# Gated recurrence block: gate, output and sum stores move from SyncE's queue to those of ScalarE and GpSimd, and a weight moves to another ring

## The chip, the core and the metric

The kernel runs on one core of a Trainium2 chip. Its time is the device time of one execution in microseconds; each kernel is run several times and the median is taken. A profile is one more execution, recorded by the hardware profiler.

The engines are TensorE (PE, with PEld for its weight loads), VectorE (DVE), ScalarE (ACT), GpSimd (POOL) and SyncE (SP). Each works through its own instructions in order and waits at semaphores. A DMA is started by an instruction on the queue of SP, ACT or POOL; if that instruction has to wait, everything behind it on the same queue waits too.

## The reference

One decoder block over 1024 tokens of width 1024, in float32. What matters here is the mixer:

```python
proj = x @ w_in                   # q | f | i | og | pool_v | gate_a | gate_b
f = lb + (1 - lb) * sigmoid(f_pre);  k = 1 - f
o = hgrn2_chunked(q, k, i, log f)              # 8 heads of 128, S_t = diag(f_t) S_(t-1) + k_t v_t^T
o = o * rsqrt(mean(o*o) + eps) * g * sigmoid(og)
a = o @ w_a
pooled = causal_multiscale_pool(pool_v)        # 4 groups, windows 2, 4, 8, 16
b = (pooled @ w_pool per group) * pool_scale
mix = (sigmoid(gate_a) * a + sigmoid(gate_b) * b) @ w_out
x = LN(alpha * x + mix);  x = LN(alpha * x + relu(x @ w_up)**2 @ w_down)
```

## The kernel before

Every float32 operand is split in two parts: ACT casts the high part (L118), DVE subtracts it from the source for the low part (L119), and PE makes three products of the parts (L201, L203, L204; in `mm3` L105, L106, L107). The big products are made in pairs of 128 output columns by a scheme with seven block products instead of eight (`pair`); `run` issues them, `takes` are the functions that receive a finished block: a gate's `put` applies the sigmoid (L696) and stores the tile to DRAM (L699 gates a and b, as `ga` and `gb`; L680 the output gates `og`).

A loop over 8 heads, two halves of 512 tokens each, makes the recurrence `hgrn(h, u)`. It begins with the decay `fd` in the ring `tA` (a scan on DVE, L811; reciprocals L817). GpSimd takes every sixteenth column of it as `T` (L819) and makes a few small tiles of that (to L838). DVE, ACT and PE go on with them: the transposes L870, ACT's copy L872, the state product L875, DVE's state `st` (L880, L883), the scores L887 and L898, their masked copy `att` (L905), the output products L915 and L918. ACT then squares (L923), takes a root (L924) and scales (L928); PE transposes (L931); DVE multiplies by the gate into the gate's own tile `og` (L932), which is stored to DRAM as `o` (L933).

Between the heads stand other pieces, listed in `EXTRAS`: `pooled` makes the window means and stores them as `po` (L754); `gates`; `o_sums` loads four tiles of `o` (L594), makes sums of them on DVE (L608 to L611) and stores them as `s1` to `s4` (L613) for the later product with w_a; `pool_products` loads a group's w_pool (L716) and its pooled tiles (L594), splits both, multiplies them (L105 to L107), scales by the gate on DVE (L729) and stores `pb` (L730). The pooled tiles use the rings `og` and `v`, the split of w_pool `q` and `f`. The rings named here have two buffers each (`tA`, `og`, `v`, `raw`; `q` and `f` have three); a tile that takes a buffer waits until the last use of the tile before it there, a store's landing among them.

A scheduler sets the order on each engine from the dependences, the priorities and its own estimate of when things are ready; after that the order is fixed. The last recurrence, head 7's second half, has a high priority. All stores and loads named here are on SP's queue.

## Time and profile before

| | us |
|---|---|
| three runs | 1462.3, 1462.83, 1464.97 |
| median | 1462.83 |
| profiled execution | 1460.19 |
| its span in the profile | 1458.5 |
| busy: PE, DVE, ACT, POOL | 1436.4, 1141.6, 758.3, 58.6 |

The span is the time from the first to the last instruction that the profiler recorded; the rest of the execution's time lies around it. [...] In the rows of the profile, a line such as L118 is the line of the kernel, `w<-og` is what is written and read, by the names of the tiles without their numbers; the granted clock (PEclk) is 1.00 when TensorE runs at full speed.

### The profile page before, as it was taken

Reading aid. Unit: us, or ns where it says so; the run is one execution under the profiler, and the core shown is the slowest. Engines: PE = TensorE matmul, PEld = TensorE weight load, DVE = VectorE, ACT = ScalarE, POOL = GpSimd, SP = SyncE. Lnnn points to the kernel's source line nnn. Section 1 sums busy time; section 2 is a strip of 40 time slices with the busy share of each in tenths; the row PEclk is TensorE's granted clock in tenths of the full one; section 3 lists DMA queues with packets and bytes.
Section 4 is the critical chain, followed back from the end, with each engine's and each line's share of the span. In section 5 each row is a group of like instructions: output and inputs, shape, how many; then the busy total and the mean of one; then the engine's idle time right before and its main releaser. Section 6 shows DMA issues by size and latency. Waiting matters only on the chain.

```text
span 1458.5 us, 20662 instructions
## 1 busy us (share of the span) xinstructions
PE 1436.4 (98%) x7377; PEld 1187.9 (81%) x7377; DVE 1141.6 (78%) x1838; ACT 758.3 (52%) x1383; POOL 58.6 (4%) x244
## 2 busy tenths in 40 slices
PE   8999999999999998999999999999999999999997
PEld 7888888888888886788888878888888888888886
DVE  5967989899898885768985597666666787777977
ACT  5445565666656655556542376555555443333535
POOL 0001001001000010000002100000000100000000
PEclk9999999999999999999999999999999999999999
DMA  7232233323234447897672225444474874445322
GB/s 253 70 126 87 85 98 101 109 75 114 90 99 138 152 132 249 301 299 241 223 247 99 73 94 195 159 146 144 152 261 149 275 260 150 153 141 163 130 73 116
DMA packets 160615, 226.82 MB, mean 156 GB/s; under 512 B 11232, under 2 KB 84480, under 8 KB 160512
## 3 DMA queue, kind: packets, MB, share of 16 engines
q1 hardware_dynamic: 158576, 218.93, 44.7%
q0 software_dynamic: 1152, 4.19, 0.8%
q10 hardware_dynamic: 784, 2.38, 0.5%
q8 instruction: 58, 0.95, 0.3%
q14 instruction: 45, 0.37, 0.1%
HBM read 154.16 MB, written 71.30 MB: 155 GB/s over the span
## 4 chain that ended last, share of the span: by engine, by line
PE 94%; DVE 3%; DMA 1%; ACT 1%; issue 0%; SPq 0%; DVEq 0%
PE ps_pj L201 16%; PE ps_pj L203 16%; PE ps_pj L204 16%; PE ps_pj L1283 4%; PE ps_pj L1285 4%; PE ps_pj L1284 4%; PE ps_pj L106 3%; PE ps_pj L107 3%; PE ps_pj L105 2%; PE ps_tr L1285 1%; PE ps_tr L1283 1%; PE ps_tr L1284 1%; PE ps_sc L201 1%; PE ps_sc L203 1%; PE ps_sc L204 1%; PE ps_hg L203 1%
## 5 line engine op out<-in xcount | busy, mean ns | idle before, releaser
L201 PE MATMUL ps_pj<-act,w 128*128 128x512 f32 x1068 | 421.6, 395 | 0.4 <-ACT act L123 0.2
L203 PE MATMUL ps_pj<-act,w 128*128 128x512 f32 x1068 | 415.1, 390 | 0.5 <-DVE act L124 0.5
L204 PE MATMUL ps_pj<-act,w 128*128 128x512 f32 x1068 | 414.1, 390 | 0.0
L201 PEld LDWEIGHTS ps_pj<-act,w 128*128 128x128 f32 x1068 | 200.6, 188 | 42.8 <-ACT act L123 0.6
L204 PEld LDWEIGHTS ps_pj<-act,w 128*128 128x128 f32 x1068 | 200.5, 188 | 42.3
L203 PEld LDWEIGHTS ps_pj<-act,w 128*128 128x128 f32 x1068 | 200.6, 188 | 40.6 <-DVE act L124 0.9
L118 ACT CAST w<-t 128x512 fp32r<-128x512 f32 x170 | 104.7, 620 | 105.0 <-PE ps_pj L203 53.8
L118 ACT CAST w<-raw 128x512 fp32r<-128x512 f32 x143 | 88.2, 620 | 117.3 <-PE ps_pj L203 62.5
L119 DVE TENSOR_TENSOR w<-raw,w 128x512 fp32r<-128x512 f32 x143 | 99.8, 702 | 55.2 <-ACT w L118 53.9
L119 DVE TENSOR_TENSOR w<-t,w 128x512 fp32r<-128x512 f32 x170 | 115.9, 685 | 29.6 <-ACT w L118 29.4
L1245 ACT CAST act<-act 128x1024 fp32r<-128x1024 f32 x66 | 66.9, 1050 | 107.9 <-issue 35.0
L1246 DVE TENSOR_TENSOR act<-act,act 128x1024 fp32r<-128x1024 f32 x66 | 79.3, 1220 | 18.5 <-ACT act L1245 15.8
L1285 PE MATMUL ps_pj<-act,act 128*128 128x512 f32 x240 | 92.9, 389 | 0.0
L1284 PE MATMUL ps_pj<-act,act 128*128 128x512 f32 x240 | 92.9, 389 | 0.0
L1283 PE MATMUL ps_pj<-act,act 128*128 128x512 f32 x240 | 92.4, 389 | 0.0
L275 DVE TENSOR_TENSOR c<-c,ps_pj 128x512 f32<-128x512 f32 x95 | 64.5, 681 | 18.0 <-PE ps_pj L204 13.4
L271 ACT COPY c<-ps_pj 128x512 f32<-128x512 f32 x96 | 55.2, 582 | 12.8 <-PE ps_pj L204 12.8
L817 DVE RECIPROCAL tC<-tA 128x128 f32<-128x128 f32 x64 | 54.1, 904 | 0.0
L1284 PEld LDWEIGHTS ps_pj<-act,act 128*128 128x128 f32 x240 | 45.1, 188 | 9.4
L1285 PEld LDWEIGHTS ps_pj<-act,act 128*128 128x128 f32 x240 | 45.1, 188 | 9.4
L1283 PEld LDWEIGHTS ps_pj<-act,act 128*128 128x128 f32 x240 | 45.1, 188 | 9.3
L241 DVE TENSOR_TENSOR t<-raw,raw 128x512 f32<-128x512 f32 x43 | 29.6, 689 | 21.9 <-DMA raw<-in_w_in_dram 19.7
(415 smaller groups left out, 2719.8 us busy)
## 6 DMA issues: line engine op xcount, KB each, us to landing
h<-c SPq DMA_DIRECT2D x106, 256.0 KB, 2.1
act<-h SPq DMA_DIRECT2D x78, 256.0 KB, 2.9
raw<-in_w_in_dram SPq DMA_DIRECT2D x64, 256.0 KB, 3.4
draw<-in_w_down_dram SPq DMA_DIRECT2D x16, 1024.0 KB, 7.8
raw<-in_w_up_dram SPq DMA_DIRECT2D x30, 512.0 KB, 4.2
raw<-in_w_in_dram SPq DMA_DIRECT2D x18, 512.0 KB, 4.0
hf<-h SPq DMA_DIRECT2D x34, 256.0 KB, 2.9
c<-o SPq DMA_DIRECT2D x24, 256.0 KB, 3.4
```

Source lines behind the costliest of these rows:

```text
L118: A.copy(hi, src)
L119: V.tensor_sub(lo, src, f(hi))
L201: PE.matmul(ps, wh[:, k], th, start=first and k == 0, stop=False, skip_group_check=True)
L203: PE.matmul(ps, wh[:, k], tl, start=False, stop=False, skip_group_check=True)
L204: PE.matmul(ps, wl[:, k], th, start=False, stop=k == CH - 1, skip_group_check=True)
L271: A.copy(t, ps)
L275: V.tensor_add(t, t, ps)
L1245: A.copy(hi, src)
L1246: V.tensor_sub(lo, src, f(hi))
L1283: PE.matmul(ps, hh[:, w], wh, start=fresh and n == 0, stop=False, skip_group_check=True)
L1284: PE.matmul(ps, hh[:, w], wl, start=False, stop=False, skip_group_check=True)
L1285: PE.matmul(ps, hl[:, w], wh, start=False, stop=n == M - 1, skip_group_check=True)
```

## The change

The stores of the gates go to ACT's queue. The stores of `o`, of the pooled tiles `po`, of the sums and of `pb`, and o_sums' loads, go to GpSimd's. The load of w_pool stays on SP, but its tile is taken from the ring `tA` instead of `raw`, which the weights of the big products use.

```diff
--- before.py
+++ after.py
@@ -589,9 +589,9 @@
         nc.sync.dma_start(out=raw, in_=rows_of)
         return raw
 
-    def loaded(src, tile_of):
+    def loaded(src, tile_of, queue=None):
         t = tile_of()
-        nc.sync.dma_start(out=t, in_=src)
+        (queue or nc.sync).dma_start(out=t, in_=src)
         return t
 
     def o_operand(name):
@@ -604,13 +604,13 @@
 
     def o_sums(kp, tile_of=c_tile):
 
-        a11, a21, a12, a22 = (loaded(od[k][u], tile_of) for k, u in ((kp, 0), (kp, 1), (kp + CH, 0), (kp + CH, 1)))
+        a11, a21, a12, a22 = (loaded(od[k][u], tile_of, nc.gpsimd) for k, u in ((kp, 0), (kp, 1), (kp + CH, 0), (kp + CH, 1)))
         V.tensor_add(a22, a21, a22)
         V.tensor_sub(a21, a11, a21)
         V.tensor_sub(a11, a22, a11)
         V.tensor_sub(a12, a12, a11)
         for name, t in zip(("s3", "s2", "s1", "s4"), (a21, a11, a22, a12)):
-            nc.sync.dma_start(out=osd[name][kp], in_=t)
+            nc.gpsimd.dma_start(out=osd[name][kp], in_=t)
 
     hg_scope = ExitStack()
     hgp = hg_scope.enter_context(tc.tile_pool(name="hgp", bufs=1, reuse_waits="tile"))
@@ -677,7 +677,7 @@
                 def put(t):
                     s = c_late() if src else t
                     A.activation(s, t, AF.Sigmoid)
-                    nc.sync.dma_start(out=dst, in_=s)
+                    nc.scalar.dma_start(out=dst, in_=s)
                 return put
 
             run(pair(
@@ -696,7 +696,7 @@
                     A.activation(s, t, AF.Sigmoid)
                     if more_of is not None:
                         V.tensor_mul(s, s, more_of)
-                    nc.sync.dma_start(out=dst if more is None else more, in_=s)
+                    (nc.scalar if more is None else nc.gpsimd).dma_start(out=dst if more is None else more, in_=s)
                 return put
 
             more = pbd[j] if spare else (None, None)
@@ -712,7 +712,7 @@
             def room(dtype=F32):
                 return tt(next(tags), dtype)
 
-            raw = raw_tile().rearrange("p k n c -> p (k n c)")[:, : 2 * 2 * P].rearrange("p (k c) -> p k c", c=2 * P)
+            raw = tt("tA").rearrange("p (k c) -> p k c", c=2 * P)
             nc.sync.dma_start(out=raw, in_=w_pool[g].rearrange("(k p) c -> p k c", p=P))
             wh, wl = split(raw, lambda: room(F32R).rearrange("p (k c) -> p k c", c=2 * P))
             for u in range(2):
@@ -727,7 +727,7 @@
                         A.activation(t, ps, AF.Copy, scale=pscale[:, j : j + 1])
                     else:
                         V.scalar_tensor_tensor(t, ps, pscale[:, j : j + 1], t, ALU.mult, ALU.mult)
-                    nc.sync.dma_start(out=pbd[j][u], in_=t)
+                    nc.gpsimd.dma_start(out=pbd[j][u], in_=t)
 
         def pooled(g):
 
@@ -751,7 +751,7 @@
                     V.scalar_tensor_tensor(pv[:, n:], cur[:, n:], 1.0 / win, pv[:, n:], ALU.mult, ALU.subtract)
 
             def put(c, i, u):
-                nc.sync.dma_start(out=pod[j + i][u], in_=c[:, HALO:])
+                nc.gpsimd.dma_start(out=pod[j + i][u], in_=c[:, HALO:])
 
             wide = [[None, None], [None, None]]
             before = small("bef", [P, HALO])
@@ -930,7 +930,7 @@
             for c in range(CH):
                 PE.transpose(pt[:, c * P : (c + 1) * P], on[:, c * P : (c + 1) * P], ident)
             V.scalar_tensor_tensor(og, pt, g_col[:, h : h + 1], og, ALU.mult, ALU.mult)
-            nc.sync.dma_start(out=od[h][u], in_=og)
+            nc.gpsimd.dma_start(out=od[h][u], in_=og)
             return st
```

The scheduler makes a new order from this on all engines. SP has 521 rows instead of 652, POOL 317 instead of 235. Two places of it follow; a name's first number is the tile's.

On SP, around the load of the first pooled tile of `pool_products` (`og_1178` from `po0_0`). The `c` tiles are gates or o_sums' operands, `o7_0` is the output of head 7's first half. Before:

```order
L594 DMA v_1181_6348<-po1_0_964 128x512
L699 DMA gb4_1_955<-c_1162_6258 128x512
L933 DMA o7_0_912<-og_1068_5768 128x512
L699 DMA ga4_1_939<-c_1160_6240 128x512
L594 DMA c_1172_6322<-o2_1_903 128x512
L594 DMA tF_1144_6163<-o7_0_912 128x512
L699 DMA gb4_0_954<-c_1170_6317 128x512
L594 DMA c_1173_6324<-o6_0_910 128x512
L594 DMA og_1178_6342<-po0_0_962 128x512
```

After:

```order
L594 DMA v_1181_6348<-po1_0_964 128x512
L716 DMA tA_1175_6336<-in_w_pool_dram 128x2x256
L594 DMA q_1184_6354<-gb0_0_946 128x512
L594 DMA q_1194_6388<-gb0_1_947 128x512
L594 DMA f_1186_6365<-gb1_0_948 128x512
L594 DMA f_1196_6399<-gb1_1_949 128x512
L716 DMA tA_1223_6555<-in_w_pool_dram 128x2x256
L594 DMA og_1178_6342<-po0_0_962 128x512
L594 DMA v_1191_6382<-po1_1_965 128x512
```

The stores of gates and outputs are gone from between `v_1181` and `og_1178`, and o_sums' loads too; w_pool's loads and the loads of the gates `gb` stand there now.

On DVE, around the scan of head 7's second half (`tA_1119`); `att0` is head 7's first half's, L608 to L611 are the second o_sums. Before:

```order
L860 TENSOR_TENSOR k64_1081_5809<-tE_1078_5800,p32_1072_5781 128x4x32
L865 TENSOR_TENSOR tC_1083_5816<-tE_1078_5800,ek_1076_5792 128x512
L119 TENSOR_TENSOR w_1113_5984<-t_1101_5933,w_1112_5983 128x512
L811 SCALAR_TENSOR_TENSOR tA_1119_6040<-starts_1016,f_1028_5542 128x256 x2
L119 TENSOR_TENSOR w_1115_6018<-raw_1093_5892,w_1114_6017 128x512
L817 RECIPROCAL tC_1120_6044<-tA_1119_6040 128x128 x4
L841 TENSOR_TENSOR q_1034_5583<-q_1034_5583,tA_1119_6040 128x512
L905 COPY_PREDICATED att0_1019<-cmask_79,sc_1021 128x512
L925 RECIPROCAL ss_1008_5439<-ss_1008_5439 128x4
L608 TENSOR_TENSOR c_1066_5756<-c_1064_5752,c_1066_5756 128x512
L119 TENSOR_TENSOR w_1149_6182<-raw_1146_6175,w_1148_6181 128x512
```

After:

```order
L608 TENSOR_TENSOR c_1066_5756<-c_1064_5752,c_1066_5756 128x512
L609 TENSOR_TENSOR c_1064_5752<-c_1063_5750,c_1064_5752 128x512
L119 TENSOR_TENSOR w_1153_6201<-raw_1147_6176,w_1152_6200 128x512
L610 TENSOR_TENSOR c_1063_5750<-c_1066_5756,c_1063_5750 128x512
L905 COPY_PREDICATED att0_1019<-cmask_79,sc_1021 128x512
L811 SCALAR_TENSOR_TENSOR tA_1119_6040<-starts_1016,f_1028_5542 128x256 x2
L611 TENSOR_TENSOR c_1065_5754<-c_1065_5754,c_1063_5750 128x512
L925 RECIPROCAL ss_1008_5439<-ss_1008_5439 128x4
L817 RECIPROCAL tC_1120_6044<-tA_1119_6040 128x128 x4
L841 TENSOR_TENSOR q_1034_5583<-q_1034_5583,tA_1119_6040 128x512
L275 TENSOR_TENSOR c_1108_5974<-c_1108_5974,ps_pj_1096_5901 128x512
```

The scan and the reciprocals now follow the copy into `att0` and L608, L609 and L610, and two L241 and two L119 of the next gates' weights. On POOL the copy `T_1121` of this scan, which followed head 7's first half's small tiles directly, now stands behind three loads of that o_sums, the store of `o6_0`, and the stores of `s1`, `s3` and `s2`.

On DVE again, at the end of head 7's first half (`og_1068` is the tile that L933 stores as `o7_0`). Before:

```order
L925 RECIPROCAL ss_1089_5872<-ss_1089_5872 128x4
L275 TENSOR_TENSOR c_1162_6258<-c_1162_6258,ps_pj_1150_6185 128x512
L275 TENSOR_TENSOR c_1160_6240<-c_1160_6240,ps_pj_1161_6242 128x512
L932 SCALAR_TENSOR_TENSOR og_1068_5768<-ps_tr_1091_5884,prm_120,og_1068_5768 128x512
L883 SCALAR_TENSOR_TENSOR st_1137_6098<-st_1087_5830,dec_1124_6055,ps_hg_1136_6094 128x128
```

After:

```order
L925 RECIPROCAL ss_1089_5872<-ss_1089_5872 128x4
L275 TENSOR_TENSOR c_1162_6258<-c_1162_6258,ps_pj_1150_6185 128x512
L119 TENSOR_TENSOR f_1177_6339<-tA_1175_6336,q_1176_6338 128x512
L275 TENSOR_TENSOR c_1160_6240<-c_1160_6240,ps_pj_1161_6242 128x512
L932 SCALAR_TENSOR_TENSOR og_1068_5768<-ps_tr_1091_5884,prm_120,og_1068_5768 128x512
L883 SCALAR_TENSOR_TENSOR st_1137_6098<-st_1087_5830,dec_1124_6055,ps_hg_1136_6094 128x128
```

The subtraction for the first w_pool (`f_1177`, from `tA_1175`) now stands between the two L275, ahead of L932; ACT's cast for it (`q_1176`) stands behind the four L928 of this half, and the store of a gate (`gb4_1`) now stands on ACT ahead of L872.

## The prediction

> **What bounds the kernel now.** I read the page first, for the bound; then the windows, for the place where the bounding engine is not busy; then the waits and the timelines of that place. The page's span, its busy line of the engines, and the shares of the chain of work that ended last:
>
> ```profile
> span 1458.5 us, 20662 instructions
> ...
> PE 1436.4 (98%) x7377; PEld 1187.9 (81%) x7377; DVE 1141.6 (78%) x1838; ACT 758.3 (52%) x1383; POOL 58.6 (4%) x244
> ...
> PE 94%; DVE 3%; DMA 1%; ACT 1%; issue 0%; SPq 0%; DVEq 0%
> ```
>
> TensorE is idle for 1458.5 − 1436.4 = 22 us in all, and the change removes no matmul. So a gain can come only out of idle time or out of matmuls that ran slowly, and a loss only out of new idle time. One stage holds what the change can reach. Windows (us, then busy time of PE, PEld, DVE, ACT, POOL, then granted clock, DMA share, GB/s), a coarse pair and then the stage cut finer:
>
> ```profile
> 560.00:600.00 40.00, 33.25 (x155) 26.57 (x154) 20.54 (x35) 18.45 (x47) 0.00 (x0) 0.91 0.74 242
> 600.00:640.00 40.00, 40.00 (x177) 32.67 (x176) 24.45 (x39) 20.36 (x35) 0.00 (x0) 1.00 0.96 321
> ```
>
> ```profile
> 575.00:577.80 2.80, 1.66 (x14) 1.67 (x15) 1.14 (x4) 0.00 (x0) 0.00 (x0) 1.00 0.97 285
> 577.80:582.80 5.00, 0.39 (x4) 0.20 (x2) 2.64 (x4) 1.76 (x9) 0.00 (x0) 0.90 0.92 324
> 582.80:588.80 6.00, 5.91 (x14) 4.01 (x15) 2.22 (x4) 5.53 (x12) 0.00 (x0) 0.51 0.59 185
> 588.80:592.00 3.20, 2.36 (x13) 1.67 (x11) 3.19 (x6) 0.39 (x1) 0.00 (x0) 1.00 0.66 246
> ```
>
> PE loses 40 − 33.25 = 6.75 us there, and the granted clock is 0.51 for 6.0 us, in which 6.0 × 0.49 = 2.9 us of work is lost. Ceiling of the gain: 9.7 us. What PE waits for, from the waits and its timeline (start, duration, instruction, idle time before it in brackets):
>
> ```profile
> PE ps_pj L105 <- ACT w L118: 4.7, 1, 4.7
> PE ps_hg L915 <- DVE st L883: 1.2, 1, 1.2
> ```
>
> ```profile
> 564.71 0.39 PE L918 MATMUL ps_hg<-st,tA 128*128 128x128 f32 x2
> ...
> 574.10 0.83 PE L875 MATMUL ps_hg<-v,tH 128*128 128x128 f32 x6
> 576.14 0.49 PE L915 MATMUL ps_hg<-v,att 128*128 128x128 f32 x2 [1.21 <-DVE st L883]
> ...
> 577.80 0.39 PE L918 MATMUL ps_hg<-st,tA 128*128 128x128 f32 x2
> 582.85 1.22 PE L105 MATMUL ps_pj<-w,q 128*128 128x512 f32 x2 [4.66 <-ACT w L118]
> ...
> 588.96 0.71 PE L105 MATMUL ps_pj<-w,q 128*128 128x512 f32 x2
> ...
> 590.97 0.50 PE L106 MATMUL ps_pj<-w,q 128*128 128x512 f32 x1 [0.84 <-DVE w L119]
> ```
>
> At 564.7 PE finishes the recurrence of head 7's first half, at 577.8 that of its second; at 582.85 the first pool product starts, 4.66 us late, and at 588.96 the third. It waits for ACT's cast of the first pooled tile, and the cast for that tile's load. SyncE's queue and ScalarE's timeline:
>
> ```profile
> 564.90 0.34 SPq L594 DMA_DIRECT2D v<-po  x1
> 573.10 0.34 SPq L699 DMA_DIRECT2D gb<-c  x1
> 573.53 0.38 SPq L933 DMA_DIRECT2D o<-og  x1
> ...
> 577.18 0.48 SPq L594 DMA_DIRECT2D og<-po  x1
> ```
>
> ```profile
> 571.15 1.28 ACT L696 ACT_TABLE_LOAD   x1
> ...
> 572.98 0.46 ACT L872 COPY tH<-ps_tr 128x384 f32<-128x384 f32 x1
> ...
> 578.28 0.28 ACT L923 ACTIVATE tH<-ps_hg 128x128 f32<-128x128 f32 x1 [3.39 <-PE ps_hg L918]
> ...
> 582.18 0.62 ACT L118 CAST w<-og 128x512 fp32r<-128x512 f32 x1 [2.75 <-DMA og<-po]
> ...
> 584.82 1.13 ACT L928 ACTIVATE tH<-ps_hg,ss 128x128 f32<-128x128 f32 x4
> ```
>
> SP issues nothing from 565.24 to 573.10: the gate store at its head waits for a sigmoid. The load of the pooled tile, og<-po, goes out at 577.18 and lets ACT start at 582.18, 5.0 us later.
>
> **The change part by part.** *The gate stores leave SP.* What stood before og<-po goes to other queues. The load does not become free at 565, though: its og slot is the one that L932 of head 7's first half writes and the L933 store reads, so it must wait for that store to land, and the store is now GpSimd's. *The weight of w_pool in the tA ring* adds to the same chain: its tile is free only after the recurrence's L918 at 564.7, so its split, done long before in the old order, now stands on ACT between L928 and the table load, and on DVE between the two L275 ahead of L932. DVE's rows:
>
> ```profile
> 569.87 1.44 DVE L275 TENSOR_TENSOR c<-c,ps_pj 128x512 f32<-128x512 f32 x2
> 571.55 0.75 DVE L932 SCALAR_TENSOR_TENSOR og<-ps_tr,prm,og 128x512 f32<-128x512 f32 x1 [0.24 <-PE ps_tr L931]
> ...
> 590.24 0.68 DVE L119 TENSOR_TENSOR w<-og,w 128x512 fp32r<-128x512 f32 x1
> ```
>
> ACT's cast of w_pool (0.62, by the L118 row) ends near 571.8; DVE's subtraction (0.68) near 572.4, the second L275 (half of 1.44) near 573.1, L932 (0.75) near 573.9, where it ended at 572.3. So the store goes out at 573.9 instead of 573.53. Landings (median us from issue):
>
> ```profile
> o<-og SPq DMA_DIRECT2D x16, 256.0 KB, 2.1
> ...
> og<-po SPq DMA_DIRECT2D x8, 256.0 KB, 3.9
> ...
> raw<-in_w_pool_dram SPq DMA_DIRECT2D x4, 256.0 KB, 4.1
> ```
>
> ```profile
> act<-x POOLq DMA_DIRECT2D x7, 512.0 KB, 6.7
> y<-x POOLq DMA_DIRECT2D x1, 512.0 KB, 9.1
> ```
>
> ```profile
> L1293 POOL DMA_DIRECT2D act<-x x7 | 3.9, 559 | 331.0 <-DVE c L275 324.2 <-PE ps_pj L204 6.3
> ```
>
> From GpSimd no 256 KB store is in the trace. It costs at least the 2.1 us that SP's take; the spread of GpSimd's own landings, 9.1 − 6.7 = 2.4, is the other end, with 0.56 us to issue it. I take 2.6, near the short end, as these landings are twice the bytes: landed at 576.5, og<-po out at 576.5 (0.7 earlier), and by its median of 3.9 instead of 5.0, since the queue behind it is shorter, usable at 580.4 (579 to 582). L118 to L105 takes 582.85 − 582.18 = 0.67: PE starts at 581.1 instead of 582.85.
>
> *ACT before that:* cast and one DMA issue (0.5 + 0.34) now stand ahead of L872, which ended 0.66 before L875 needed it: L875 and all up to L918 come 0.3 later, and L918 ends near 578.5. PE's idle time becomes 2.6 us instead of 4.66. *Does the clock hold?* These rows of the start show an idle time near that length:
>
> ```profile
> 9.28 0.66 PE L162 MATMUL ps_sc<-ident,x 128*128 128x128 f32 x4 [1.92 <-DMA x<-in_x_dram]
> ```
>
> ```profile
> 8.00:13.00 5.00, 3.72 (x21) 3.22 (x22) 3.25 (x9) 2.55 (x7) 0.00 (x0) 1.00 1.03 380
> ```
>
> After 1.92 us it stayed at 1.00; in the stage the mean of 0.90 over 577.8 to 582.8 puts the fall one us before 582.8, 3.6 us after PE stopped. An idle time of 2.6 lies between; I take it as holding.
>
> *What is late next* is ACT. After the cast at 580.4 come the four L923 (1.15 us, 578.28 to the end of the group), the cast of the second tile, and table load to the end of L928, which took 582.81 to 585.95, 3.1 us. That ends at 580.95 + 1.15 + 0.55 + 3.1 = 585.8. Then L931 on PE (0.7), L932 (0.75) and the subtraction (0.68) on DVE put the third product's L106 at 587.9, where it was 590.97. **Stage: −3.0 us** (−1.5 with the load usable at 582, −4.8 at 578.6).
>
> *The recurrence on GpSimd.* L819, the copy T, now stands behind o_sums' loads and stores in three places. Heads 4 and 6 are given room by the new order (PE's part of head 6 is 11 to 16 us later). Head 7's second half is the tight one: T waits behind three s stores, and DVE's scan behind L608 to L610.
>
> ```profile
> 534.70:541.00 6.30, 6.30 (x34) 5.23 (x35) 6.30 (x11) 4.80 (x15) 2.03 (x10) 1.00 0.81 236
> 541.00:564.00 23.00, 23.00 (x162) 18.86 (x161) 17.23 (x35) 11.90 (x24) 0.00 (x0) 1.00 0.66 209
> ```
>
> The scan, four reciprocals, L841, L905 and L925, all but 0.1 of the 6.3 us of DVE's first row, move into the second, from which about 2.7 (a subtraction, two L241, L608) go forward and 0.7 (w_pool's split) leaves: 17.2 + 6.2 − 3.4 = 20.0 of 23 us busy. DVE finishes head 7's st with about 3 us in hand before L918 at 564. I charge **+0.5** (0 to 3, and not below nothing, as PE is at 23.00 of 23.00).
>
> *Elsewhere:* in head 2 L875 now follows L870 directly and needs L872 between them (0.46 and two hand-overs, near 0.9); ACT takes 46 DMA issues of 0.34, beside 52% of work. **+1.0** (0 to 3). Pooled tiles and later pool products are read long after their stores: nothing. From 600 PE is 40.00 of 40.00 busy at a DMA share of 0.96; nothing is gained there, and the 3 us are kept, as the loads behind it are issued earlier too.
>
> Sum: −3.0 + 0.5 + 1.0 = **−1.5 us**. The profiled execution took 1460.19 us (1.7 around the span) and becomes 1458.7; the median of the runs shown is 2.6 higher, 1462.83, and becomes 1461.3.
>
> The Trainium skill, "DMA: Bandwidth & Descriptors", section "Issuing engines are not separate DMA queues", says that starting DMAs on several engines saves only the time to initiate them. By it the three gate stores ahead of og<-po are worth 3 × 0.34 = 1.0 us, and the sum would be 1460.2 + 0.5. The trace disagrees where a queue stands still behind a store that waits: 565.24 to 573.10.
>
> **The rivals.** I call 0.2%, 2.9 us, what a measurement of this kernel can tell from no change.
>
> A, the forecast, 0.36; by its bounds −4.5 to +3. B: the load lands as fast as stores do, and the new order costs PE nothing: −4.8 (to −9.7 at the ceiling), 1458.0; 0.22. For it speaks the DMA share of 0.97 that the stores caused before og<-po; against it the chain through L932. C: 2.6 us idle halves the clock after all: −1.5 + 2.9 = +1.4, 1464.2; 0.12.
>
> D, slower: GpSimd's queue is in order, and T for head 7 stands behind loads that wait for gate stores to land. If those are over 3 us later than I reckon, DVE's room between 541 and 564 is gone, and L918 waits; at 4.5 us more PE idles 4.5 and the clock halves as it did after 4.66: −1.5 + 4.5 + 2.9 = +5.9, 1468.7; 0.20. Against it speaks only that room of 3 us.
>
> E, slower: GpSimd's transfers take longer to set up while DVE works. If the o store lands 2.4 us later (9.1 against 6.7), og<-po goes out at 578.9, the load is usable at 582.8, later than now; PE idles 5 us, the clock halves, the stage's −3.0 becomes +0.6, o_sums is 1 us later: near +3, 1465.9; 0.10. The Trainium skill, "SBUF — State Buffer", section "SBUF: two separate sides", has such a rule: a DMA from GpSimd waits for its descriptors while DVE runs an op that holds both ports. The trace's 559 ns for an issue show no such wait.
>
> **How the numbers follow.** Faster: a quarter of A and nearly all of B, 0.30. Slower: D, over half of E, a fifth of C and edges of A and B, 0.30. Within: 0.40. The range leaves out B's far end (1456) and D's (1469.5). A alone: 1458.3 to 1465.8.
>
> **What would show it.** Right: og<-po issued near 576.5, 2 to 3 us of idle time before L105, a granted clock of 1.00 from 577 to 589, at most 1 us of new waits ahead of 575. Wrong: a clock near 0.5 after L918 (C), idle time before head 7's L898, L915 or L918 with T or st as releaser (D), an o<-og landing over 4 us (E), or PE waits after 600.

## The result, and the profile after

The changed kernel took 1461.71 us (median of 12 runs, 1460.1 to 1465.12) beside 1462.57 us for the kernel before: ratio 0.9994, 95% interval 0.9985 to 1.0003. A second comparison on another chip gave 1461.68 beside 1462.0, ratio 1.0004 (0.9996 to 1.0013). The ratios are estimated from all the runs and are not the quotients of the two medians. The change makes no difference that can be measured. The forecast of 1461.3 lies 0.4 us from the median, and no measurable change was its likeliest case; its mechanism holds only in part.

Page of the changed kernel (span and busy line). The profiled execution took 1461.8 us. TensorE is as busy as it was, and GpSimd's busy time rose by the issues that it took over:

```profile
span 1459.6 us, 20689 instructions
...
PE 1436.3 (98%) x7377; PEld 1188.7 (81%) x7377; DVE 1141.2 (78%) x1838; ACT 758.6 (52%) x1383; POOL 104.4 (7%) x326
```

Its windows (us, then busy time of PE, PEld, DVE, ACT, POOL; then granted clock, DMA share, GB/s), first coarse, then the stage cut finer:

```profile
560.00:600.00 40.00, 33.88 (x211) 27.47 (x210) 23.05 (x41) 22.23 (x51) 9.09 (x17) 0.96 0.84 272
600.00:640.00 40.00, 40.00 (x178) 33.13 (x177) 26.15 (x41) 18.22 (x32) 5.40 (x10) 1.00 0.83 276
640.00:720.00 80.00, 79.08 (x345) 64.11 (x344) 69.72 (x112) 46.49 (x85) 4.32 (x8) 1.00 0.77 266
```

```profile
576.30:581.60 5.30, 2.05 (x16) 1.86 (x16) 2.25 (x4) 0.00 (x0) 2.23 (x5) 1.00 1.00 309
581.60:583.00 1.40, 0.72 (x2) 0.30 (x2) 0.74 (x2) 1.39 (x8) 0.00 (x0) 0.99 0.96 364
583.00:586.50 3.50, 3.50 (x9) 2.78 (x9) 1.43 (x3) 3.23 (x10) 0.54 (x1) 0.52 0.92 330
```

The clock still falls: to 0.52, for 3.5 us instead of 6.0, so 3.5 × 0.48 = 1.7 us are lost there instead of 2.9. The DMA engines are at a share of 1.00 from 576.3 to 581.6, where TensorE stands still. PE's waits, and its timeline (start, duration, instruction, idle time before it in brackets):

```profile
PE ps_pj L105 <- ACT w L118: 3.7, 1, 3.7
PE ps_pj L106 <- DVE w L119: 1.2, 1, 1.2
PE ps_hg L875 <- ACT tH L872: 0.7, 1, 0.7
PE ps_pj L201 <- ACT room L271: 0.6, 1, 0.6
```

```profile
574.50 0.83 PE L875 MATMUL ps_hg<-v,tH 128*128 128x128 f32 x6
576.53 0.49 PE L915 MATMUL ps_hg<-v,att 128*128 128x128 f32 x2 [1.21 <-DVE st L883]
...
578.20 0.39 PE L918 MATMUL ps_hg<-st,tA 128*128 128x128 f32 x2
582.28 0.77 PE L105 MATMUL ps_pj<-w,q 128*128 128x512 f32 x2 [3.70 <-ACT w L118]
...
589.43 0.50 PE L106 MATMUL ps_pj<-w,q 128*128 128x512 f32 x1 [1.22 <-DVE w L119]
```

The third product's L106 comes at 589.43 where it came at 590.97. Why L105 still waits 3.70 us, from the timelines of GpSimd, SyncE and ScalarE, and from the DMA issues of 573 to 582 us (count, KB, median us from issue to landing):

```profile
573.27 0.54 POOL L933 DMA_DIRECT2D o<-og  x1 [8.56 <-DVE og L932]
```

```profile
576.33 0.32 SPq L594 DMA_DIRECT2D og<-po  x1
```

```profile
581.61 0.62 ACT L118 CAST w<-og 128x512 fp32r<-128x512 f32 x1 [6.21 <-DMA og<-po]
```

```profile
s<-c POOLq DMA_DIRECT2D x3, 256.0 KB, 6.0
...
c<-o POOLq DMA_DIRECT2D x2, 256.0 KB, 4.1
o<-og POOLq DMA_DIRECT2D x1, 256.0 KB, 3.0
...
og<-po SPq DMA_DIRECT2D x1, 256.0 KB, 5.3
```

The load goes out at 576.33, 0.85 us earlier than before, and takes 5.3 us. The loads and stores of the sums, which stood ahead of it and behind it on SyncE's queue, now run beside it from GpSimd's.

### The profile page after: what moved, and what is told of

Read it like the earlier page. It is cut to its first block, busy times and chain, and to the rows that moved or that the text cites. A ratio compares the mean times of both kernels' runs of the same rounds, so it can differ in the third digit from the quotient of the medians.

```text
span 1459.6 us, 20689 instructions
## 1 busy us (share of the span) xinstructions
PE 1436.3 (98%) x7377; PEld 1188.7 (81%) x7377; DVE 1141.2 (78%) x1838; ACT 758.6 (52%) x1383; POOL 104.4 (7%) x326
## 3 DMA queue, kind: packets, MB, share of 16 engines
q0 software_dynamic: 7712, 25.70, 4.9%
q10 hardware_dynamic: 7408, 14.44, 2.7%
## 4 chain that ended last, share of the span: by engine, by line
PE 94%; DVE 3%; DMA 1%; ACT 1%; issue 0%; SPq 0%; DVEq 0%; ACTq 0%
PE ps_pj L201 16%; PE ps_pj L203 16%; PE ps_pj L204 16%; PE ps_pj L1284 4%; PE ps_pj L1285 4%; PE ps_pj L1283 4%; PE ps_pj L106 3%; PE ps_pj L107 3%; PE ps_pj L105 3%; PE ps_tr L1284 1%; PE ps_tr L1285 1%; PE ps_tr L1283 1%; PE ps_sc L201 1%; PE ps_sc L204 1%; PE ps_sc L203 1%; PE ps_hg L204 1%
## 5 line engine op out<-in xcount | busy, mean ns | idle before, releaser
L201 PE MATMUL ps_pj<-act,w 128*128 128x512 f32 x1068 | 421.0, 395 | 0.9 <-ACT room L271 0.6
L201 PEld LDWEIGHTS ps_pj<-act,w 128*128 128x128 f32 x1068 | 200.5, 188 | 43.2 <-ACT room L271 1.0
L119 DVE TENSOR_TENSOR w<-raw,w 128x512 fp32r<-128x512 f32 x143 | 99.4, 699 | 56.9 <-ACT w L118 55.9
L119 DVE TENSOR_TENSOR w<-t,w 128x512 fp32r<-128x512 f32 x170 | 116.0, 686 | 31.6 <-ACT w L118 31.3
L275 DVE TENSOR_TENSOR c<-c,ps_pj 128x512 f32<-128x512 f32 x95 | 64.7, 681 | 24.2 <-PE ps_pj L204 18.5
L241 DVE TENSOR_TENSOR t<-raw,raw 128x512 f32<-128x512 f32 x43 | 29.6, 688 | 20.4 <-DMA raw<-in_w_in_dram 20.1
```

What stands on the lines that cost most here:

```text
L119: V.tensor_sub(lo, src, f(hi))
L201: PE.matmul(ps, wh[:, k], th, start=first and k == 0, stop=False, skip_group_check=True)
L275: V.tensor_add(t, t, ps)
```

## The experiments

The theory after the result: og<-po is issued earlier, but shares the 16 DMA engines with the sums' loads and stores, and so lands late; what is saved ahead of L105 is then eaten by waits behind it. The rivals: GpSimd's transfers or ScalarE's issues themselves cost time; the ring costs time by its split in ACT's and DVE's chain; or the parts gain separately and other work is simply late anyway. Ratios below are to the kernel before, with the 95% interval.

**The parts, one by one.** First the changed kernel with the ring undone:

```diff
-            raw = tt("tA").rearrange("p (k c) -> p k c", c=2 * P)
+            raw = raw_tile().rearrange("p k n c -> p (k n c)")[:, : 2 * 2 * P].rearrange("p (k c) -> p k c", c=2 * P)
```

> The changed kernel with one part undone: w_pool's weight is back in the raw ring; gates stay on ScalarE's queue, outputs and sums on GpSimd's. Theory 1 (the DMA engines, at a share of 1.00 from 576.3 to 581.6 in the changed kernel, set when the first pooled tile is usable): the split of w_pool no longer stands ahead of L932 and L872, so the o store and og<-po go out about 0.7 earlier, near 575.6, and two of the 256 KB w_pool loads leave the stretch from 571 to 582; og<-po lands in 4 to 4.5 us instead of 5.3, PE idles 2 to 3 us before L105, the clock holds: 2 to 3 us faster than the changed kernel, ratio to before 0.997 to 0.9985. Rival (the chain through L932 and the store alone sets it, the transfer takes 5.3 as before): 0.7 us faster than the changed kernel, idle time near 3.0, ratio near 0.999. Rival 2 (the ring was the part that helped, the raw ring is short): slower than before, with PE waits at L201 to L204 after 600.

Measured: 1462.7 us, 0.9996 (0.9988 to 1.0005). PE's timeline:

```profile
580.64 0.73 PE L105 MATMUL ps_pj<-w,q 128*128 128x512 f32 x2 [1.72 <-ACT w L118]
584.57 0.50 PE L106 MATMUL ps_pj<-w,q 128*128 128x512 f32 x1 [1.54 <-DVE w L119]
587.71 0.73 PE L105 MATMUL ps_pj<-w,q 128*128 128x512 f32 x2 [1.51 <-ACT w L118]
```

The first wait shrinks to 1.72 us and the clock stays at 1.00, but the product behind it waits twice, and L201 waits 1.52 us for room at 695.77 (0.57 in the changed kernel). Next the kernel before with only the gate stores on ScalarE:

```diff
-                    nc.sync.dma_start(out=dst, in_=s)
+                    nc.scalar.dma_start(out=dst, in_=s)
...
-                    nc.sync.dma_start(out=dst if more is None else more, in_=s)
+                    (nc.scalar if more is None else nc.sync).dma_start(out=dst if more is None else more, in_=s)
```

> The kernel before with one part of the change: gates stored by ScalarE's queue, all else on SP as before. Theory 1: SP no longer stands still behind a gate store until 573.10, og<-po goes out 0.5 to 1.5 earlier than 577.18 (it still waits for the o store and the loads ahead of it), but the same transfers share the DMA engines: usable near 581 to 582, idle 3 to 4.5 before L105, clock halved for some us; ratio 0.998 to 1.000. Rival (SP's standing still is the cost): og<-po near 574, idle near 1, clock 1.00, ratio near 0.995.

Measured: 1465.47 us, 1.0016 (1.0007 to 1.0025). PE's timeline and two windows:

```profile
580.97 1.22 PE L105 MATMUL ps_pj<-w,q 128*128 128x512 f32 x2 [2.78 <-ACT w L118]
...
605.11 1.22 PE L105 MATMUL ps_pj<-w,q 128*128 128x512 f32 x2 [3.99 <-ACT w L118]
```

```profile
577.00:581.00 4.00, 1.22 (x12) 1.03 (x10) 2.81 (x5) 1.82 (x10) 0.00 (x0) 0.90 1.03 369
581.00:588.00 7.00, 6.96 (x19) 4.79 (x20) 3.25 (x6) 5.77 (x12) 0.00 (x0) 0.57 0.58 194
```

Here the clock was halved before 2.78 us of idle time were over: the forecast's 2.6 that "holds" stood too near. The gain of 1.9 us ahead of L105 is lost again to a wait of 3.99 us at 605. Ahead of that wait ScalarE stands 5.97 us for the weight of the second group of pool products, which goes out from the ring raw at 595.51 and takes 5.4 us:

```profile
600.95 0.62 ACT L118 CAST q<-raw 128x512 fp32r<-128x512 f32 x1 [5.97 <-DMA raw<-in_w_pool_dram]
```

Then the kernel before with only the ring changed (the diff of the first experiment, the other way round):

> The kernel before with only w_pool's weight moved to the tA ring, all stores on SP. Theory 1: w_pool's split stands ahead of L932 and L872, SP still stands behind the gate store, og<-po goes out 0.5 to 1.5 later than 577.18, idle before L105 5 to 6 us, clock halved: 0.5 to 3 us slower, ratio 1.000 to 1.002. Rival (the raw ring was short): faster, by earlier weight loads, ratio below 0.999.

Measured: 1462.1 us, 0.9997 (0.9988 to 1.0006): og<-po goes out at 578.04, 0.86 us later than before, and L105 waits 4.43 us. Last, the kernel before with only outputs, sums and pooled tiles on GpSimd's queue (`nc.sync` to `nc.gpsimd` at L613, L730, L754, L933, the loads of `o_sums`, and the `more` stores of L699):

> The kernel before with one part of the change: outputs, sums and pooled tiles on GpSimd's queue; gates on SP, w_pool in the raw ring. Theory 1: SP still stands behind a gate store until 573, but og<-po is next behind it and waits only for the o store (on GpSimd, landing near 575.5), so it goes out near 575.5 and shares the DMA engines: idle before L105 2 to 3.5 us; ratio 0.998 to 1.000. If the clock falls after an idle time near 2.8 as with the gates alone, the whole gain at the stage is lost again: ratio 0.9995 to 1.0015. Rival (GpSimd's queue makes the recurrence of head 7 late): idle time before L898, L915 or L918 ahead of 575, slower by over 0.2%.

Measured: 1468.02 us, 1.0031 (1.002 to 1.0041). Waits of PE:

```profile
PE ps_pj L105 <- ACT q L118: 4.4, 1, 4.4
PE ps_pj L105 <- ACT w L118: 3.3, 1, 3.3
PE ps_pj L201 <- ACT w L118: 2.5, 3, 1.1
```

og<-po goes out at 575.80, the wait ahead of L105 is 3.28 us, and a new one of 4.41 us stands at 645.66. So no part gains alone; the two queue parts alone lose 0.16% and 0.31%, together they stand at 0.9996.

**The first pooled tile in another ring**, so that its load needn't wait for head 7's store (the changed kernel, w_pool's weight back in raw):

```diff
+                early = (lambda: (next(tags), tt("tA"))[1]) if g == u == 0 else room
-                pl = [split(loaded(pod[2 * g + i][u], room), row_tile) for i in range(2)]
+                pl = [split(loaded(pod[2 * g + i][u], room if i else early), row_tile) for i in range(2)]
```

> The changed kernel with w_pool's weight back in the raw ring, and the first pooled tile (po0_0) in the tA ring instead of the og ring: it is loaded near 565, after L918 of head 7's first half, and no longer waits for the o store. Theory 1 and its rivals on the wait agree that the first product no longer waits: idle before L105 under 0.5, no halved clock. If nothing is late behind it, 5 to 7 us faster than before, ratio 0.995 to 0.9965. Rival (the wait moves to the second pair of pooled tiles, og<-po of po0_1, which still waits for the o store and shares the DMA engines): PE runs the first two products by 581 and idles 2 to 4 us there, the clock may halve, 2 to 4 us faster, ratio 0.997 to 0.9985.

Measured: 1465.41 us, 1.0019 (1.001 to 1.0028). The schedule put the first products ahead of head 7's L875, at 574; the next pooled tile then came later than ever, og<-po at 579.30, and the third product's L105 waits 7.03 us at 584.62. Moving one load moved the wait.

**The sums later, by their place in the code:**

```diff
-            ("gates", 4), ("o_sums", 2), ("pool_products", 0), ("gates", 5),
+            ("gates", 4), ("pool_products", 0), ("o_sums", 2), ("gates", 5),
```

> The changed kernel with the third o_sums moved behind the first pool_products, so that its loads and stores (two loads and three stores of 256 KB on GpSimd's queue from 573.8 to 580) leave the stretch in which the first pooled tile is loaded. Theory 1 (the DMA engines, at a share of 1.00, set how long that load takes): og<-po lands in 3 to 4.2 us instead of 5.3, idle before L105 1.4 to 2.6 us instead of 3.70, clock at 1.00 or halved for less than 2 us: 1.5 to 4 us faster than the changed kernel at this place, ratio 0.9965 to 0.9985, unless the sums are late for the product with w_a after 660. Rival (the transfer takes 5 us whatever runs beside it, or what counts is when it is issued): landing near 5.3, idle near 3.7, ratio as the changed kernel, 0.9985 to 1.0003.

Measured: 1463.37 us, 0.9996 (0.9986 to 1.0007). The edit did not do what it says: the scheduler kept the sums' transfers where they were, so this run tests nothing of the theory. It shows a spread instead: og<-po, issued at 576.18, let ACT start at 582.63, 6.4 us later; the wait ahead of L105 was 5.41 us.

**Other work for TensorE in the stage:** gates 5 ahead of pool_products 0, in the changed kernel and in the kernel before:

```diff
-            ("gates", 4), ("o_sums", 2), ("pool_products", 0), ("gates", 5), ("pool_products", 1),
+            ("gates", 4), ("o_sums", 2), ("gates", 5), ("pool_products", 0), ("pool_products", 1),
```

> The changed kernel with gates 5 issued ahead of the first pool_products, so that PE has products with weights (L201, L203, L204) ready while the first pooled tile is on its way. Theory 1 (the stage's loss is TensorE without work, 6.1 us idle between 560 and 600 and 1.7 us by the halved clock): both go, 5 to 8 us faster than before, ratio 0.9945 to 0.9965, clock 1.00 from 560 to 600. Rival (ScalarE and VectorE bind, the wait only moves to the later pool products): new waits L105 <- ACT after 600, ratio 0.998 to 1.001.

> The kernel before (all on SP's queue, w_pool in the raw ring) with gates 5 issued ahead of the first pool_products. Theory 1: the 6.75 us idle and the 2.9 us of halved clock go as well, and with them all that the change could reach: 5 to 9 us faster than before, within 2 us of the changed kernel with the same edit. Rival (SP standing still behind a gate store also makes the weights of gates 5 and the later pooled tiles late, so that the queues matter once PE has work): 3 us or more slower than the changed kernel with the same edit.

Measured: 1462.6 us, 0.9998 (0.9989 to 1.0007), and with the old queues 1467.71 us, 1.0031 (1.0019 to 1.0042). PE's timeline of the first, its windows, and the DVE row behind the first of the waits:

```profile
607.79 0.50 PE L105 MATMUL ps_pj<-w,q 128*128 128x512 f32 x1 [2.73 <-ACT q L118]
616.72 0.77 PE L201 MATMUL ps_pj<-act,w 128*128 128x512 f32 x1 [3.20 <-DVE q L729]
```

```profile
560.00:600.00 40.00, 38.03 (x237) 30.95 (x236) 23.57 (x41) 24.22 (x55) 8.13 (x15) 1.00 0.77 242
600.00:640.00 40.00, 34.07 (x143) 27.45 (x142) 24.30 (x38) 14.37 (x26) 6.39 (x12) 0.96 0.86 283
```

```profile
603.91 0.69 DVE L608 TENSOR_TENSOR tC<-tE,tC 128x512 f32<-128x512 f32 x1 [4.31 <-DMA tC<-o]
```

From 560 to 600 only 2.0 us of idle time are left and the clock stays at 1.00, but 5.9 us are lost in the next 40 us instead. DVE stands 4.31 us at the last sums, whose load flies late, with the splits for TensorE behind it. In this order the queues and the ring together do matter: the old ones are some 5 us slower (1.0031 against 0.9998). Which of the two it is was not taken apart.

**The sums held back, and this time held.** A GpSimd copy that needs the first pooled tile's low part stands ahead of the four loads; two loads and three stores leave the stretch in which og<-po flies (lines behind 719 are four further on: L919 is L915, L922 is L918):

```diff
+                if g == u == 0:
+                    mark = G.tensor_copy(small("mark", [P, 1], 1), f(pl[0][1])[:, :1])
+                    with tc.issue_after(mark.ins):
+                        o_sums(2)
...
-            ("gates", 4), ("o_sums", 2), ("pool_products", 0),
+            ("gates", 4), ("pool_products", 0),
```

> The changed kernel with the third o_sums (four loads, four stores of 256 KB) held back on GpSimd until the first pooled tile has been split: a small GpSimd copy of that tile's low part stands ahead of the four loads. Lines behind 719 stand four further on (L915 is L919, L918 is L922, L923 is L927). Theory (the transfer og<-po took 5.3 us from its issue because it shared the 16 DMA engines with the sums' two loads and three stores, share 1.00): without them og<-po lands 4.2 us or less after its issue at 576.3 (usable by 580.5 to 581), TensorE is idle 2.6 us or less ahead of the first L105 instead of 3.70, the DMA share from 576.3 to 581.6 falls below 0.7; the kernel comes out at 0.9985 to 0.9995 of the kernel before, unless the sums, now later, hold DVE elsewhere. Rival (the load is slow in itself: rows of 2 KB spread over its own queue, whatever else flies): it lands 5 us or more after the issue again, idle 3.5 to 4.5, ratio 0.9990 to 1.0000. Second rival: the sums come too late, L608 waits on DVE at 590 to 610 and TensorE waits for the splits behind it: 1.000 to 1.002.

Measured: 1460.8 us beside 1463.79, 0.9981 (0.9972 to 0.9989), the only version that is faster than the kernel before by more than the interval. Its SyncE, ScalarE, GpSimd and PE rows, and three windows: that of the theory, the flight of og<-po itself, and the stretch behind the second wait:

```profile
576.12 0.32 SPq L594 DMA_DIRECT2D og<-po  x1
```

```profile
579.00 0.62 ACT L118 CAST w<-og 128x512 fp32r<-128x512 f32 x1 [3.05 <-DMA og<-po]
```

```profile
580.64 2.16 POOL L594 DMA_DIRECT2D c<-o  x4
```

```profile
579.67 0.73 PE L105 MATMUL ps_pj<-w,q 128*128 128x512 f32 x2 [0.43 <-ACT w L118]
...
585.91 0.74 PE L105 MATMUL ps_pj<-w,q 128*128 128x512 f32 x2 [1.37 <-ACT w L118]
```

```profile
576.30:581.60 5.30, 3.98 (x23) 3.19 (x24) 1.86 (x5) 2.58 (x11) 1.69 (x4) 1.00 0.70 228
576.12:579.00 2.88, 1.81 (x16) 1.81 (x16) 0.95 (x3) 0.00 (x0) 0.55 (x1) 1.00 0.81 262
587.00:591.00 4.00, 4.00 (x11) 3.13 (x12) 3.13 (x6) 1.56 (x3) 0.54 (x1) 0.57 0.88 340
```

Issued 0.2 us earlier than in the changed kernel, the same load lands within 579.00 − 576.12 = 2.9 us instead of 5.3, and L105 waits 0.43 us. What was held back is not missed: 600 to 640 is 40.00 of 40.00 busy. The ratio is below the range that the theory gave, the share of 0.70 at its bound; by the rival the load would have taken 5 us or more again. Over its own flight, up to 579.00, the share is 0.81; the 0.70 also counts the time behind its landing. The clock still falls, though the longest wait behind L918 is 1.37 us: at 0.57 from 587 to 591 it costs 4.0 × 0.43 = 1.7 us, as much as in the changed kernel.

The edit makes a new order on all engines, so other transfers move too. In the changed kernel the next pooled tile (578.39) and the weight of the third group of pool products (578.82) also go out while og<-po flies; here they go out at 579.05 and 579.48, when it has landed. With the ring undone, where the sums fly but no such weight does, the load took at most 579.97 − 575.76 = 4.2 us. With outputs, sums and pooled tiles alone on GpSimd's queue, three loads of the sums went out in the 1.9 us behind og<-po, their stores only from 582.67, and it took at most 578.52 − 575.80 = 2.7 us. The pair that differs least has the weight in raw both times: 4.2 us with the sums in flight, 2.8 us with the sums held (the run with the weight back in raw, below). So the traffic beside the load makes it late, the sums by at least 1.4 us of it; how much falls to their loads and how much to their stores is not shown.

Beside it ran the order with gates 5 first once more, with the last sums taken out of the recurrence's priority and held behind pool_products 1:

```diff
+        def last_sums(_):
+            tags = iter(("tD", "tE", "tF", "tC"))
+            with tc.issue_after(last[-1]):
+                o_sums(CH - 1, lambda: tt(next(tags)))
...
-                    if (h, u) == (HEADS - 1, 1):
-                        tags = iter(("tD", "tE", "tF", "tC"))
-                        o_sums(h - CH, lambda: tt(next(tags)))
...
+            ("gates", 4), ("o_sums", 2), ("gates", 5), ("pool_products", 0), ("pool_products", 1), ("last_sums", 0),
```

> The changed kernel with gates 5 ahead of pool_products 0, and with the last o_sums taken out of the recurrence's priority: called behind pool_products 1, its DVE steps held behind the last multiply of pool_products 1. Lines behind 699 stand some seven further on (L729 is L736, L915 is L922). Theory (with gates 5 first the stage at 576 to 583 loses nothing, and the two waits of 2.73 and 3.20 us at 607 to 617 of that order came from DVE standing 4.31 us at L608 of the last sums, which it must do in order ahead of the splits that TensorE waits for): both waits fall under 1 us, 560 to 640 keeps TensorE busy over 78 us of 80 (76.1 fell out of 80 with gates 5 first alone: 38.03 + 38.00 at most), and the kernel comes out at 0.996 to 0.998 of the kernel before. Rival (the waits come from the loads for the products, which fly late whatever DVE does, q<-gb above all): the waits stay at 2 us or more each, ratio 0.999 to 1.000. Second rival: the last sums, later, are late for the w_a or w_out stage that reads s1 to s4, and TensorE waits behind 640: 1.000 to 1.003.

Measured: 1462.86 us, 0.9992 (0.9984 to 1.0001). (The 76.1 us in the expectation is a slip: the two windows above give 38.03 + 34.07 = 72.10.) The waits at 607 and 616 fall to 1.23 and 0.81 us and TensorE is busy 75.76 of 80 us, so DVE's stand was part of it. But DVE now stands 6.22 us at a split whose tile an earlier store still reads:

```profile
608.30 0.69 DVE L119 TENSOR_TENSOR f<-tA,q 128x512 fp32r<-128x512 f32 x1 [6.22 <-DMA pb<-f]
```

Of the time, less than half of what was expected came; neither theory nor rival as put.

**The ring, where the engines are free:** the kernel with the sums held, and w_pool's weight back in raw (the first experiment's diff on top).

> The changed kernel with the third o_sums held behind the first pooled tile's split, as in the run before, and with w_pool's weight back in raw_tile's ring: the ring part of the change undone where the 16 DMA engines are free of the sums. Theory (the gain came from freeing the engines for og<-po; the ring adds nothing once that transfer is early): og<-po lands 4.2 us or less after its issue, idle ahead of the first L105 under 1 us, ratio to the kernel before 0.9975 to 0.9990, its interval overlapping that of the run with the ring. Rival (the two parts need each other: with the weight in raw the split's ACT steps come at other times and wait later, as the run with the ring alone undone had 1.54 and 1.51 us at 584 to 588 and 1.52 at 696): ratio 0.9990 to 1.0000.

Measured: 1464.63 us beside 1462.0, 1.0012 (1.0002 to 1.0022). The theory fell, and the rival went further than it said. PE, ACT and SP:

```profile
579.87 0.73 PE L105 MATMUL ps_pj<-w,q 128*128 128x512 f32 x2 [0.63 <-ACT w L118]
...
603.18 1.22 PE L105 MATMUL ps_pj<-w,q 128*128 128x512 f32 x2 [3.80 <-ACT w L118]
```

```profile
600.95 0.62 ACT L118 CAST q<-raw 128x512 fp32r<-128x512 f32 x1 [3.31 <-DMA raw<-in_w_pool_dram]
```

```profile
593.98 0.38 SPq L716 DMA_DIRECT2D raw<-in_w_pool_dram  x1
```

The first wait is as short as with the ring, so that part of the theory stands a second time (ACT's cast starts 2.8 us after the issue at 576.36). But the weight of the second group goes out at 593.98 and lands 6.9 us later, and PE waits 3.80 us for what is behind its split. In the kernel before the same load goes out at 594.12 and takes 3.4 us. The two rows, this run's first, from the DMA issues (count, KB, median us from issue to landing):

```profile
raw<-in_w_pool_dram SPq DMA_DIRECT2D x1, 256.0 KB, 6.9
```

```profile
raw<-in_w_pool_dram SPq DMA_DIRECT2D x1, 256.0 KB, 3.4
```

In this run the four stores of the held sums are issued from 591.08 to 595.53, and from 593.98 to 600.95 the DMA share is 0.95: what was held back for the first load now flies beside this one. In the run with the sums held and the ring, the weight of the second group is

```profile
571.75 0.38 SPq L716 DMA_DIRECT2D tA<-in_w_pool_dram  x1
```

out 22.2 us earlier, and nobody waits for it. The changed kernel itself, once more beside these:

> The changed kernel itself once more, on the chip and beside the runs of before of this call: against the run with the sums held it tells whether holding them gains in a like comparison. Theory (og<-po is late by the sums' traffic): idle ahead of the first L105 3.5 us or more, ratio 0.9985 to 1.0000, above that with the sums held by 0.0005 or more. Rival (the spread of the landing is chance): idle anywhere from 2 to 4 us, ratio as low as 0.9980, like the run with the sums held.

Measured: 1461.68 us, 1.0004 (0.9996 to 1.0013); L105 waits 4.35 us at 584.41 and og<-po takes 5.6 us. Its interval lies above that of the kernel with the sums held; that of the first comparison (0.9985 to 1.0003) overlaps it at the edge (0.9985 to 0.9989). The two kernels were compared through the kernel before, not side by side.

## Why the prediction was right, and where not

*The number.* By the prediction's own signs its mechanism came out partly wrong: 3.70 us of idle time instead of 2 to 3, a clock near 0.5 after L918, waits behind 600. As the traces have them, its three terms are −1.5, 0 and +1.5 us instead of −3.0, +0.5 and +1.0. The interval of the measured change runs from −2.2 to +0.4 us and holds the forecast as well as no change at all. That 1461.3 lies so near the median is therefore in part luck.

*Right: what bounds it, and when the load goes out.* Nothing but idle time and slow matmuls moved: PE is 1436.3 us busy beside 1436.4. The load og<-po went out at 576.33 (forecast 576.5), held by the store of head 7's first half, which landed 3.0 us after GpSimd issued it (forecast 2.6). So the landing was slower, and its issue, at 573.27, earlier than the forecast's 573.9; the two misses cancel.

*Wrong: "by its median of 3.9 instead of 5.0, since the queue behind it is shorter, usable at 580.4".* It took 5.3, 5.6 and 6.4 us in three profiles of the same transfers. The queue behind the load was shorter, as forecast, and the load took no less; what counted in these runs is what else flies. From 573.8 to 580.4 GpSimd issues two loads and three stores of the third sums. Five times 256 KB at the 309 GB/s of the window are 4.2 us of all 16 engines, which is an upper estimate of what they cost the load, since the stores land only after it (6.0 us). Holding them back made it at most 2.9 us, in two kernels. The stage's term is therefore −1.5 us (L106 at 589.43 instead of 590.97), not −3.0; the lower end, "−1.5 with the load usable at 582", is what came. Of the 1.5 us by which L106 missed its forecast of 587.9, 1.2 are the load (581.6 instead of 580.4). The Trainium skill, "DMA: Bandwidth & Descriptors", section "Issuing engines are not separate DMA queues", says that DMAs of all issuing engines run on the same 16 engines and interleave: the prediction weighed its rule on initiation alone, and this part of it is what the trace bears out.

*Unsupported: that 2.6 us of idle time hold the clock.* In the changed kernel 3.70 us came, so it wasn't put to the test there. The prediction went by the 3.6 us from TensorE's stop to the fall in the kernel before. That time is not fixed: with gates alone the clock fell some 2.0 us after the stop (0.90 over 577 to 581 puts the fall at 580.2, the stop is 578.19), after a gap of 1.21 us a little earlier; in the changed kernel it fell 4.4 us after it (578.58 to 583.0). With the sums held it fell behind waits of 0.43, 0.30, 1.37 and 0.30 us, while with the ring undone it held through waits of 1.72, 1.54 and 1.51. So no length of idle time read from one place forecasts it here, and what does stays open. The Trainium skill, "TensorE: Matmul & The Clock Gate", section "Part 1: The HAM clock gate (the "warmup" mystery)", gives about 3.4 us of idleness as the time after which it falls. The run's 2.78 disagrees if it is counted alone, and so does the run with the sums held.

*Right: what is late next.* The chain through ACT's L928 and DVE's split holds the third product (1.22 us ahead of L106). With the first wait shorter it costs more: 1.54 and 1.51 us with the ring undone.

*The recurrence on GpSimd, forecast +0.5:* no wait ahead of head 7. The rows of st and T (DVE's timeline; GpSimd's):

```profile
561.26 0.34 DVE L883 SCALAR_TENSOR_TENSOR st<-st,dec,ps_hg 128x128 f32<-128x128 f32 x1
```

```profile
545.60 0.61 POOL L819 COPY T<-tA 128x32 f32<-128x32 f32 x1 [1.03 <-DVE tA L811]
```

st ends at 561.60, 2.8 us ahead of the first L918 at 564.37 ("about 3 us in hand"). The rival of a late T is out, and that of slow GpSimd transfers too: 3.0 us against the 5.0 that it needed.

*Elsewhere, forecast +1.0:* 0.7 us at head 2's L875 (forecast 0.9), and 79.85 − 79.08 = 0.8 us more idle time from 640 to 720, where the forecast saw nothing to lose.

*The sum.* Idle time of PE from 570 to 720 plus what the halved clock costs, by each timeline, and 0.7 for L875: 6.9 + 2.9 = 9.8 us before; 6.9 + 1.7 + 0.7 = 9.3 after; 4.6 + 1.7 + 0.7 = 7.0 with the sums held. The differences, −0.5 and −2.8 us, stand beside 1461.71 − 1462.57 = −0.9 and −0.3 us measured for the change and −3.0 for the sums held. Single spans do not show this: 1458.5, 1459.6 and 1459.7 us.

*Not seen at all: what the ring is for.* The prediction counted only the split that it puts into ACT's and DVE's chain. Its worth is 1.0012 against 0.9981, each beside the kernel before: with it the second weight is there before it is needed. From the ring raw that weight goes out between 592.8 and 595.5, and how long it takes then differs: at most 3.2 us with the ring undone, where nobody waited for it, 5.4 us with the gates alone and 6.9 us with the sums held, where TensorE waited 3.99 and 3.80 us. So the ring could look useless with the sums where they were, and was worth about 0.3% with the sums moved onto that weight's flight. That the traffic beside it makes the difference is argued from these flights, not shown by a run of its own.

What stays open: why outputs and sums on GpSimd alone cost 0.31%. The trace puts 4.41 us of it at 645.66 on a cast that comes after a pooled tile's late load; it wasn't taken apart further. Open too: what makes the clock fall after short waits, and how the lateness of og<-po divides between the sums' loads and their stores.

## What to carry to other kernels

When a load is late, look at the DMA share of the window in which it flies before reckoning with its median: moving instructions to another queue changes when it is issued, and everything else that is set free at the same moment shares the engines with it. Hold back the transfers that nobody waits for yet, and look at what they fly beside afterwards. Here queues, ring and holding back together were worth 0.19%, the queues and the ring without it nothing that could be measured. Parts that gain nothing one by one can still need each other, so undo a part again in the best version before it is called useless.

## What the runs showed of the hardware

- The load og<-po (256 KB) let ScalarE start at most 2.7, 2.8 and 2.9 us after its issue where the mean DMA share of that stretch was 0.56, 0.83 and 0.81 (outputs and sums alone on GpSimd; sums held with the weight in raw; sums held). It took 4.2 to 4.5 us at 0.85 to 0.98 (ring undone, ring alone, gates alone) and 5.0 to 6.4 us at 0.90 to 1.00 (the kernel before; the changed kernel twice; the run with the sums' place in the code changed).
- The clock fell around idle times of 2.78, 3.28, 3.70 us and more, but with the sums held also after none longer than 1.37 us, and it held through 1.72, 1.54 and 1.51 us with the ring undone. In the changed kernel it fell only 0.7 us after TensorE had started again. At half rate it stayed 3.4 us in the changed kernel and with the sums held, and 6.8 us with the gates alone.
- A store of 256 KB from GpSimd took 0.54 us to issue and a median of 2.3 us to land (o<-og of the whole changed kernel), about what SyncE's took (2.1); ScalarE's issue of a gate took 0.33 us.
- The DMAs that ScalarE starts run on a queue of their own, q10: it moved 2.38 MB in the kernel before and 14.44 MB in the changed one, which are the 46 gate stores of 256 KB more. GpSimd's queue q0 went from 4.19 to 25.70 MB.
